# A hybrid trunk layer: another unit of seven products in each of three weight products, and half of their low-half subtractions on GpSimd

## The chip, the core and the metric

The kernel runs on one core of one Trainium2 chip. The time is that of one execution on the device, in microseconds. The kernel before takes 1451.33 us, the median of three runs (1449.8 to 1453.53). One execution was also recorded by the hardware profiler; every duration below is from that record.

## What is computed

One layer of a decoder for 256 tokens of width 2048, in float32. The change touches the step in which two attention branches are merged: columns of the input projection give gates, and the gates weigh the two branches' output projections.

```python
h = rms_norm(x, norm_mix_pre)
# w_in: columns 3392 to 5439 are the gates of branch A, 5440 to 7487 those of branch B
gates = h @ w_in[:, 3392:7488]
g = sigmoid(gates).reshape(B, S, 2, 2048)
merged = g[:, :, 0] * (o_a @ w_o_mla) + g[:, :, 1] * (o_b @ w_o_swa)
y = merged @ w_out
```

`o_b` is the result of the sliding-window attention, `w_o_swa` its 2048x2048 output matrix (`wo_b` in the kernel).

## The kernel before

**Three products for one.** TensorE multiplies in a reduced float32 format (`F32R`). To keep float32 accuracy each operand is split in a high half, rounded to that format, and a low half, the rest. Each product of operands is then three matmuls, high by high, high by low and low by high (`mm3`, L195 to L198). For the weights, `convert` (L150) makes the halves: ScalarE copies the raw row block into `whi` (L161), VectorE subtracts it from the raw one to give `wlo` (L162). The halves go through a ring of four buffers each (`RING = 4`): a conversion waits until TensorE has used the one four before.

**Pairs of column blocks.** `pair_gemm` computes the product of 256 tokens with 1024 columns of weights. Tokens come in two tiles of 128, columns in two blocks of 512, and the 2048 rows of the weights in 16 blocks of 128 rows, taken two by two: eight units. An order string says for each unit of which kind it is:

- `p`, a plain unit: two row blocks, each converted at 128x1024 and multiplied with both token tiles: 2 x 2 x 2 products, 24 matmuls of 128x512.
- `s`, a unit of seven products (Winograd's form of Strassen's scheme): 21 matmuls. It needs sums and differences of the four token blocks, made ahead by `token_sums` (L378 to L388), and of the four weight blocks. GpSimd's queue loads the two row blocks (`gr`, L329 and L330), VectorE makes four 512-wide differences (`weight_sums`, L225 to L232) into `gta` and `gtb`, and four pieces are converted: the odd row block (1024 wide), half of the even one (512), `gta` and `gtb` (1024 each). At the end of the product `end_sums` adds the four sums of seven-product units back (L358 to L364).

**The stage around the change.** First comes `out_b(0)`, a plain product of the first 512 columns of `wo_b`. Then `gate_pair(0, ...)` and `gate_pair(2, ...)`, two pairs for the 2048 gates of branch B, and `out_pair`, a pair for columns 512 to 1535 of `wo_b`. The last 512 columns (`out_b(3)`) follow later, mixed with the next stage. A gate pair ends with four additions from PSUM (L838) and four tanh on ScalarE (L839); `gated` (L796, L797) multiplies the gate with the branch and stores the result from GpSimd's queue. `out_pair` ends with four additions from PSUM (L857) and four `gated`.

**What sets the order.** The instructions of VectorE, ScalarE and SyncE are put in order at build time by a planner; those of TensorE and GpSimd stand in the order of the code. Each engine works through its instructions in that order. `at(t, f)` asks for a piece of work at a tick; a unit of either kind takes two ticks. The token sums of the gates (`x_sums`) and of the output (`o_sums`) are asked for so.

Of the kernel before, what the change touches and what calls it, by code (L numbers as in the profile page):

```python
# [11 lines left out]
F32 = mybir.dt.float32  # L12
F32R = mybir.dt.float32r
# [3 lines left out]
ALU = mybir.AluOpType  # L17
AX = mybir.AxisListType

P = 128  # L20
# [20 lines left out]
def trunk_layer(ctx, tc, x, x_cols_in, conv_cols_in, g_mix_post, g_ffn_post, w_in, w_q, w_kv,  # L41
                sinks, rel, wo_a, wo_b, w_out, w_up, w_down, rope_tab, out):
    nc = tc.nc
    vec, act, pe, pool = nc.vector, nc.scalar, nc.tensor, nc.gpsimd
# [10 lines left out]
    base = ctx.enter_context(tc.tile_pool(name="base", bufs=1))  # L55
    ring = ctx.enter_context(tc.tile_pool(name="ring", bufs=RING))

    def sb(pl, shape, name, dt=F32, tag=None, bufs=None):
        return pl.tile(shape, dt, name=name, tag=tag or name, **({"bufs": bufs} if bufs else {}))
# [12 lines left out]
    def warm_up(n):  # L72
        for i in range(n):
# [7 lines left out]
                       base=0, channel_multiplier=1)  # L81
# [65 lines left out]
        flex[0] = kind  # L147
        turn.update(raw=0, w=0)

    def convert(raw, n, own=None, parts=None, into=None):  # L150
        i = cnt[0]
        cnt[0] += 1
        if into:
            hi, lo = into
        elif own:
            hi, lo = (own.tile([P, 1024], F32R, name=f"w{part}{i}", tag="w" + part) for part in ("hi", "lo"))
        else:
            extra = in_turn("w")
            hi, lo = (ring_tile("w" + part, f"w{part}{i}", F32R, extra) for part in ("hi", "lo"))
        for a, b in parts or ((0, n),):  # L160
            act.copy(hi[:, a:b], raw[:, a:b])  # L161
            vec.tensor_tensor(lo[:, a:b], raw[:, a:b], hi[:, a:b].bitcast(F32), op=ALU.subtract)  # L162
        return hi, lo

    def raw_row(src, n=1024):
        i = cnt[0]
        cnt[0] += 1
        raw = new_raw(f"raw{i}")
        ins = nc.sync.dma_start(raw[:, :n], src)
        if more_raw and more_raw[-1] is raw_x and "rx" not in staged:  # L170
            staged.add("rx")
            tc.keep_in_program_order(ins)
        return raw
# [100 lines left out]
        u, p = (i, 0) if i < NA[0] else (i - NA[0], 1)  # L274
        return park_sums(f"ta{i}_", w_down, 2 * u, 1024 * p, place, t0, **kw)

    def pair_gemm(name, w, k0, c0, order, act_of, s_of, kind, d, place=None, sums=None, parked=None, held=None, into=None, tied=False):

        c11, c12, c21, c22 = c = banks(kind, f"c{name}_")
        q, used = [], set()  # L280
        row = lambda k: w[(k0 + k) * P:(k0 + k + 1) * P, c0:c0 + 1024]
# [6 lines left out]
        chunks, hold = [2 * order.count("p")], len(held) if held else 0  # L288
        left = [order.count("s")]

        def plain(u, last):
            for k in (2 * u, 2 * u + 1):
                chunks[0] -= 1
                w_ = convert(raw_row(row(k)), 1024, into=into(chunks[0]) if hold else None)
                for t in range(NT):
                    if t and chunks[0] < hold:
                        held[hold - 1 - chunks[0]] = (act_of(k, 1), w_)
                        continue
                    for j in range(2):
                        mul(c[2 * t + j], act_of(k, t), half(w_, j),  # L300
                            not (chunks[0] or (t and hold)) and (j == 1 or not left[0]))
                tick()
# [23 lines left out]
        def seven(u, last):  # L326
            s1, s2, s3, s4 = s_of(u)
            even, odd = place()
            pool.dma_start(even, row(2 * u))  # L329
            pool.dma_start(odd, row(2 * u + 1))  # L330
            ta, tb = sums()
            w_ = convert(odd, 1024)
            weight_sums(even, odd, ta, tb, tied)
            if not q:
                q[:] = banks(1 - kind, f"q{name}_")
            q1, q5, q7, q6 = q
            mul(c11, act_of(2 * u + 1, 0), half(w_, 0))
            mul(c12, s4, half(w_, 1))
            w_ = convert(even, 512)
            mul(q1, act_of(2 * u, 0), half(w_, 0), last)  # L340
            w_ = convert(ta, 1024)
            mul(q5, s1, half(w_, 0), last)
            mul(q7, s3, half(w_, 1), last)
            tick()
            w_ = convert(tb, 1024)
            left[0] -= 1
            mul(q6, s2, half(w_, 0), last)
            mul(c21, act_of(2 * u + 1, 1), half(w_, 1))
            tick()
            if last:  # L350
                end_sums()
# [17 lines left out]
        n = order.count("s")  # L369
        plain_of, seven_of = iter(range(n, len(order))), iter(range(n))  # L370
        for i, kd_ in enumerate(order):
            if kd_ == "s":
                u = next(seven_of)
# [336 lines left out]
    for g in range(4):  # L710
        acc = gemm(XH, XL, w_in, 0, KT, C_QS + 512 * g, 512)[0] if g else acc_q0
        swa_q(g, acc)
        b = now[0]
# [47 lines left out]
    acc, _ = gemm(XH, XL, w_in, 0, KT, 0, 512)  # L761
# [4 lines left out]
    acc, _ = gemm(XH, XL, w_in, 0, KT, C_KV, KVR + ROPE)  # L766
# [28 lines left out]
    def gated(j, t, g, o):  # L795
        vec.scalar_tensor_tensor(g, g, 1.0, o, op0=ALU.add, op1=ALU.mult)  # L796
        pool.dma_start(yb_d[j, t], g)  # L797
# [3 lines left out]
    esg, pg = open_pool("pg")  # L801
    xs = {}

    def x_sums(u):
        st = sb(pg, [P, 1024], f"xs{u}", F32R)
        a, m = (sb(pg, [P, 512], f"x{n}{u}", tag="x" + n, bufs=1) for n in "am")
        xs[u] = token_sums(xt[u].bitcast(F32), a, m, st[:, 0:512], st[:, 512:1024])

# [7 lines left out]
    os_ = {}  # L816

    def o_sums(u):
        st = sb(pg, [P, 1024], f"os{u}", F32R)
        a, m = (sb(pg, [P, 512], f"o{n}{u}", tag="x" + n, bufs=1) for n in "am")  # L820
        os_[u] = token_sums(ot[u].bitcast(F32), a, m, st[:, 0:512], st[:, 512:1024])

    def two_pairs(act_of, s_of, w, c0, kind, name, order, tiles):
        d = []

        def result_tiles():
            d[:] = tiles()
            return d

        c = pair_gemm(name, w, 0, c0, order, lambda k, t: tuple(x(k)[:, t * P:(t + 1) * P] for x in act_of),  # L830
                      lambda u: s_of[u], kind, result_tiles, g_place, gate_sums, tied=True)
        return c, d

    def gate_pair(j, kind, tiles, then=lambda t, g: None):
# [26 lines left out]
            finish_out(i)  # L861

    both = sb(base, [P, D], "ob0", tag="sg")
    for t, f in ((0, lambda: x_sums(0)), (3, lambda: x_sums(1)), (6, lambda: o_sums(0)), (10, lambda: x_sums(2)), (28, lambda: o_sums(1))):
        at(now[0] + t, f)
    acc = out_b(0, (pss, "s"))
    for t in range(NT):
        act.copy(both[:, t * 512:(t + 1) * 512], acc[t])
    tb1 = [sb(pg, [P, 512], f"tb1_{t}") for t in range(NT)]
    gate_pair(0, 0, lambda: [x_ for t in range(NT) for x_ in (stg(f"tb0_{t}"), tb1[t])],  # L870
              lambda t, g: gated(0, t, g, both[:, t * 512:(t + 1) * 512]))
    parked_b2 = []
    d = gate_pair(2, 1, lambda: [stg(f"tb{2 + i}_{t}") for t in range(NT) for i in range(2)])
    out_pair((tb1, d[0::2]))
# [152 lines left out]
    b = now[0] + 2  # L1027
# [5 lines left out]
    acc = out_b(3)  # L1033
# [4 lines left out]
    for j in range(4):  # L1038
        acc, _ = gemm(XH, XL, w_in, 0, KT, C_GA + 512 * j, 512)
        if j == 3:  # L1040
            both = sb(base, [P, D], "ta3", tag="sg")
        for t in range(NT):
            g = both[:, t * 512:(t + 1) * 512] if j == 3 else stg(f"ta{j}_{t}")
# [523 lines left out]
    held = [None] * 7  # L1567
# [52 lines left out]
RING = 4  # L1620
A_ORDER = "ppspspsp"
NA_ = A_ORDER.count("s")
GATE_ORDER = "ppspspsp"
OUT_ORDER = "ppsppspp"
B_ORDER = "psspsspssp"
B2_ORDER = "ppsspssppp"
NB2 = B2_ORDER.count("s")
# [74 lines left out]
```

## Time and profile before

| | |
|---|---|
| median of three runs | 1451.33 us |
| the profiled execution, in all | 1448.96 us |
| its span, first to last instruction | 1447.2 us |
| TensorE's mean granted clock | 0.998 |
| two gate pairs, first matmul to first of the output pair | 218.35 to 301.70 us |
| output pair, first to last matmul | 301.9 to 344.5 us |
| low halves on VectorE in the whole span (L162, from `raw`, `gr`, `gta`, `gtb` and others) | 491, 576.0 us |

A line of the profile's timeline gives start, duration, engine, line of the kernel, operation, output<-input without buffer numbers, shape, and in brackets the idle time before it with what ended it. Rows that follow each other without a gap on VectorE overlap a little: the step from one start to the next is shorter than the duration. PE is TensorE's matmul, DVE is VectorE, ACT ScalarE, POOL GpSimd, SP SyncE.

### The profile page before, as it was taken

To read this page: it belongs to the slowest core of one execution; us is meant where nothing else is said; L and a number is where in the kernel's file an instruction comes from. 1 tells how busy PE (TensorE), PEld (TensorE's weight loads), DVE (VectorE), ACT (ScalarE), POOL (GpSimd) and SP (SyncE) were. 2 spreads that over 40 slices of the span, in tenths; PEclk is the share of its full clock that TensorE was granted. 3 is DMA by queue.
4 is the path that set the end of the run, shared out by engine and by line. 5 is a ranking of instruction groups with operands and counts; after the bars stand their busy time and mean duration, and the time that the engine had idled before them with its cause. 6 is when DMAs were issued, how large, how long until landed. Compare 5 with 4: busy or idle time off the path is not lost.

```text
span 1447.2 us, 21393 instructions
## 1 busy us (share of the span) xinstructions
PE 1436.9 (99%) x7497; PEld 1228.8 (85%) x7497; DVE 1175.9 (81%) x2042; ACT 864.7 (60%) x1400; POOL 127.6 (9%) x240
## 2 busy tenths in 40 slices
PE   9999999999999999999999999999999999999997
PEld 7888888888888888888888888888888888888886
DVE  7788898988777775978789888986778787876798
ACT  7588875554555655546566565555656555555673
POOL 2022110000000111100000111100000100010000
PEclk9999999999999999999999999999999999999999
DMA  9655375657876779965666799987988888778965
GB/s 317 203 172 162 105 262 185 215 181 221 260 215 206 239 241 331 345 221 187 219 230 220 267 364 344 325 287 232 319 285 294 284 293 278 256 272 286 355 216 205
DMA packets 162316, 365.45 MB, mean 253 GB/s; under 512 B 21008, under 2 KB 32144, under 8 KB 162208
## 3 DMA queue, kind: packets, MB, share of 16 engines
q1 hardware_dynamic: 138192, 278.82, 57.5%
q0 software_dynamic: 23872, 85.00, 16.8%
q8 instruction: 59, 0.97, 0.3%
q14 instruction: 49, 0.40, 0.1%
q10 hardware_dynamic: 144, 0.26, 0.1%
HBM read 327.29 MB, written 36.75 MB: 252 GB/s over the span
## 4 chain that ended last, share of the span: by engine, by line
PE 55%; DVE 1%; DMA 1%; issue 0%; ACT 0%; DVEq 0%; ACTq 0%
PE ub L1395 10%; PE ua L1395 10%; PE ub L1399 5%; PE ua L1399 5%; PE cd L198 2%; PE cd L196 2%; PE cd L197 2%; PE accg L198 2%; PE accg L196 2%; PE accg L197 2%; PE cdc L198 1%; PE cdc L196 1%; PE cdc L197 1%; PE qd L198 1%; PE qd L196 1%; PE qd L197 1%
## 5 line engine op out<-in xcount | busy, mean ns | idle before, releaser
L161 ACT CAST whi<-raw 128x1024 fp32r<-128x1024 f32 (+2 forms) x491 | 496.7, 1022 | 348.6 <-PE accg L198 70.0
L162 DVE TENSOR_TENSOR wlo<-raw,whi 128x1024 fp32r<-128x1024 f32 (+2 forms) x491 | 576.0, 1186 | 146.2 <-ACT whi L161 139.7
L1395 PE MATMUL ua<-ahl,whi 128*128 128x512 f32 x640 | 154.6, 391 | 0.0
L1395 PE MATMUL ub<-ahl,whi 128*128 128x512 f32 x640 | 154.5, 391 | 0.0
L196 PE MATMUL accg<-whi,ahl 128*128 128x512 f32 (+1 forms) x352 | 137.4, 391 | 0.0
L1395 PEld LDWEIGHTS ua<-ahl,whi 128*128 128x128 f32 x640 | 117.5, 188 | 22.7
L1395 PEld LDWEIGHTS ub<-ahl,whi 128*128 128x128 f32 x640 | 117.5, 188 | 22.7
L198 PE MATMUL accg<-whi,ahl 128*128 128x512 f32 (+1 forms) x352 | 135.6, 385 | 0.0
L197 PE MATMUL accg<-wlo,ahl 128*128 128x512 f32 (+1 forms) x352 | 134.8, 383 | 0.0
L1399 PEld LDWEIGHTS ub<-ahl,wlo 128*128 128x128 f32 x640 | 82.2, 191 | 3.2
L1399 PEld LDWEIGHTS ua<-ahl,wlo 128*128 128x128 f32 x640 | 82.2, 191 | 3.1
L1399 PE MATMUL ua<-ahl,wlo 128*128 128x256 f32 x640 | 83.7, 283 | 0.0
L1399 PE MATMUL ub<-ahl,wlo 128*128 128x256 f32 x640 | 83.2, 283 | 0.0
L198 PEld LDWEIGHTS accg<-whi,ahl 128*128 128x128 f32 x352 | 66.1, 188 | 12.7
L196 PE MATMUL accg<-whi,bhl 128*128 128x512 f32 x192 | 76.0, 396 | 0.0
L197 PEld LDWEIGHTS accg<-wlo,ahl 128*128 128x128 f32 x352 | 66.2, 188 | 10.6
L196 PEld LDWEIGHTS accg<-whi,ahl 128*128 128x128 f32 x352 | 66.1, 188 | 10.6
L198 PE MATMUL accg<-whi,bhl 128*128 128x512 f32 x192 | 75.1, 391 | 0.0
L197 PE MATMUL accg<-wlo,bhl 128*128 128x512 f32 x192 | 75.0, 391 | 0.0
L161 ACT CAST whi<-xraw 128x1024 fp32r<-128x1024 f32 x34 | 35.9, 1055 | 27.5 <-PE ub L1395 11.9
L162 DVE TENSOR_TENSOR wlo<-xraw,whi 128x1024 fp32r<-128x1024 f32 x34 | 41.5, 1220 | 9.8 <-ACT whi L161 9.8
L198 PEld LDWEIGHTS accg<-whi,bhl 128*128 128x128 f32 x192 | 36.0, 188 | 7.6
(692 smaller groups left out, 2920.5 us busy)
## 6 DMA issues: line engine op xcount, KB each, us to landing
raw<-in_ffn_w_up_dram SPq DMA_DIRECT2D x142, 512.0 KB, 4.9
raw<-in_w_in_dram SPq DMA_DIRECT2D x99, 512.0 KB, 4.5
raw<-in_ffn_w_down_dram SPq DMA_DIRECT2D x64, 512.0 KB, 5.7
xraw<-in_ffn_w_up_dram SPq DMA_DIRECT2D x34, 512.0 KB, 5.5
raw<-in_w_o_swa_dram SPq DMA_DIRECT2D x28, 512.0 KB, 5.5
ta_s<-in_ffn_w_down_dram POOLq DMA_DIRECT2D x28, 512.0 KB, 6.8
ta<-ta_s POOLq DMA_DIRECT2D x28, 512.0 KB, 6.5
raw<-ta SPq DMA_DIRECT2D x28, 512.0 KB, 5.0
```

The source lines that it names most:

```text
L161: act.copy(hi[:, a:b], raw[:, a:b])
L162: vec.tensor_tensor(lo[:, a:b], raw[:, a:b], hi[:, a:b].bitcast(F32), op=ALU.subtract)
L196: pe.matmul(o, ah, bh, start=start, stop=False)
L197: pe.matmul(o, ah, bl, start=False, stop=False)
L198: pe.matmul(o, al, bh, start=False, stop=stop)
L1395: pe.matmul(acc[i], hi[:, c], hn[p][:, j * 512:(j + 1) * 512], start=p + j == 0, stop=stop)
L1399: pe.matmul(acc[i][:, 0:256], lo[:, c], hn[p][:, j * 512:j * 512 + 256], start=False, stop=False)
```

## The change

Two order strings change: the gate pairs get four units of seven products in place of three, in the order plain, plain, seven, seven, plain, seven, seven, plain; the output pair gets three in place of two. The additional token sums are made: a fourth for the gates, in a buffer that is free at that time (`rx`), and a third for the output, in the buffer of the first gate sum (`xs0`), once that has been used for the last time. And `convert` takes the engine that subtracts: in these three pairs GpSimd makes the low halves of the odd row blocks, 24 operations of 128x1024, in plain units as in the others. `ob0` is another name for the first half of the same buffer.

```diff
-    def convert(raw, n, own=None, parts=None, into=None):
+    def convert(raw, n, own=None, parts=None, into=None, low=vec):
...
             act.copy(hi[:, a:b], raw[:, a:b])
-            vec.tensor_tensor(lo[:, a:b], raw[:, a:b], hi[:, a:b].bitcast(F32), op=ALU.subtract)
+            low.tensor_tensor(lo[:, a:b], raw[:, a:b], hi[:, a:b].bitcast(F32), op=ALU.subtract)
...
-                w_ = convert(raw_row(row(k)), 1024, into=into(chunks[0]) if hold else None)
+                w_ = convert(raw_row(row(k)), 1024, into=into(chunks[0]) if hold else None, low=low if k % 2 else vec)
...
             ta, tb = sums()
-            w_ = convert(odd, 1024)
+            w_ = convert(odd, 1024, low=low)
...
     def x_sums(u):
-        st = sb(pg, [P, 1024], f"xs{u}", F32R)
+        st = sb(base, [P, 1024], "xs3", F32R, tag="rx") if u == 3 else sb(pg, [P, 1024], f"xs{u}", F32R)
...
     def o_sums(u):
-        st = sb(pg, [P, 1024], f"os{u}", F32R)
+        st = sb(pg, [P, 1024], f"os{u}", F32R, tag="xs0" if u == 2 else f"os{u}")
...
-                      lambda u: s_of[u], kind, result_tiles, g_place, gate_sums, tied=True)
+                      lambda u: s_of[u], kind, result_tiles, g_place, gate_sums, tied=True, low=pool)
...
-    for t, f in (... (10, lambda: x_sums(2)), (28, lambda: o_sums(1))):
+    for t, f in (... (10, lambda: x_sums(2)), (14, lambda: x_sums(3)),
+                 (26, lambda: o_sums(1)), (34, lambda: o_sums(2))):
         at(now[0] + t, f)
...
-GATE_ORDER = "ppspspsp"
-OUT_ORDER = "ppsppspp"
+GATE_ORDER = "ppsspssp"
+OUT_ORDER = "ppspspsp"
```

GpSimd's queue at the beginning of the first gate pair. Before, it holds only the loads of row blocks for seven-product units (`gr`), two for each unit:

```order
L329 DMA gr_2853<-in_w_in_dram 128x1024
L330 DMA gr_2853<-in_w_in_dram 128x1024
L329 DMA gr_2939<-in_w_in_dram 128x1024
L330 DMA gr_2939<-in_w_in_dram 128x1024
L329 DMA gr_3021<-in_w_in_dram 128x1024
L330 DMA gr_3021<-in_w_in_dram 128x1024
```

Now the low halves of odd row blocks stand between them, of plain units (from `raw`) and of the others (from `gr`):

```order
L329 DMA gr_2903<-in_w_in_dram 128x1024
L330 DMA gr_2903<-in_w_in_dram 128x1024
L162 TENSOR_TENSOR wlo_2792<-raw_2789,whi_2791 128x1024
L162 TENSOR_TENSOR wlo_2838<-raw_2835,whi_2837 128x1024
L162 TENSOR_TENSOR wlo_2859<-gr_2853,whi_2858 128x1024
L329 DMA gr_2995<-in_w_in_dram 128x1024
L330 DMA gr_2995<-in_w_in_dram 128x1024
L162 TENSOR_TENSOR wlo_2909<-gr_2903,whi_2908 128x1024
```

Three subtractions stand ahead of the load for the third seven-product unit, and one more ahead of that for the fourth.

VectorE at the first seven-product unit of the first gate pair. Before, between the second token row (`xa`, `xm`, `xs` for the gates, `oa`, `om`, `os` for the output) and the low half of the even row block (from `gr`, 512 wide):

```order
L162 TENSOR_TENSOR wlo_2838<-raw_2835,whi_2837 128x1024
L421 TENSOR_TENSOR os_3238<-om_3240,os_3238 128x512
L162 TENSOR_TENSOR wlo_2859<-gr_2853,whi_2858 128x1024
L230 TENSOR_TENSOR gta_2856<-gr_2853 128x512 x2
L230 TENSOR_TENSOR gtb_2857<-gr_2853,gta_2856 128x512
L162 TENSOR_TENSOR wlo_2877<-gr_2853,whi_2876 128x512
L230 TENSOR_TENSOR gtb_2857<-gr_2853,gtb_2857 128x512
```

Now:

```order
L421 TENSOR_TENSOR xs_2939<-xm_2941,xs_2939 128x512
L384 TENSOR_TENSOR om_3198<-oa_3197 128x128
L385 TENSOR_TENSOR om_3198<-oa_3197 128x128
L386 TENSOR_TENSOR om_3198<-om_3198,oa_3197 128x128
L387 TENSOR_TENSOR om_3198<-oa_3197,om_3198 128x128
L381 TENSOR_TENSOR oa_3397<-bhl_608 128x512
L162 TENSOR_TENSOR wlo_2877<-gr_2853,whi_2876 128x512
L421 TENSOR_TENSOR os_3196<-om_3198,os_3196 128x512
```

The two 1024-wide low halves are gone from here to GpSimd, the four weight sums have moved up, and the fourth gate sum (`xs_2939`) and the beginning of the third output sum (`oa_3397`) stand ahead of the even row's low half; the low half of the second output sum (`os_3196`) has come behind it.

VectorE at the end of the output pair. Before, low halves for the next product (from `raw`) stand between the additions and the gating:

```order
L857 TENSOR_TENSOR udo<-udo,co_3467 128x512
L162 TENSOR_TENSOR wlo_3866<-raw_3863,whi_3865 128x1024
L796 SCALAR_TENSOR_TENSOR tb_0_2765<-tb_0_2765,udo 128x512
L857 TENSOR_TENSOR udo<-udo,co_3468 128x512
L857 TENSOR_TENSOR udo<-udo,co_3469 128x512
L796 SCALAR_TENSOR_TENSOR tb_0_3422<-tb_0_3422,udo 128x512
L796 SCALAR_TENSOR_TENSOR tb_1_2766<-tb_1_2766,udo 128x512
L857 TENSOR_TENSOR udo<-udo,co_3470 128x512
L162 TENSOR_TENSOR wlo_3888<-raw_3884,whi_3887 128x1024
```

Now:

```order
L162 TENSOR_TENSOR wlo_3898<-raw_3895,whi_3897 128x1024
L363 TENSOR_TENSOR udo<-udo,qo_3605 128x512
L364 TENSOR_TENSOR udo<-udo,qo_3605 128x512
L857 TENSOR_TENSOR udo<-udo,co_3507 128x512
L857 TENSOR_TENSOR udo<-udo,co_3508 128x512
L796 SCALAR_TENSOR_TENSOR tb_0_2765<-tb_0_2765,udo 128x512
L796 SCALAR_TENSOR_TENSOR tb_0_3462<-tb_0_3462,udo 128x512
L857 TENSOR_TENSOR udo<-udo,co_3509 128x512
L857 TENSOR_TENSOR udo<-udo,co_3510 128x512
L796 SCALAR_TENSOR_TENSOR tb_1_2766<-tb_1_2766,udo 128x512
L796 SCALAR_TENSOR_TENSOR tb_1_3464<-tb_1_3464,udo 128x512
L162 TENSOR_TENSOR wlo_3916<-raw_3913,whi_3915 128x1024
```

The eight finishing operations stand together, and the third low half of the next product behind all of them.

More of the change, by code (lines that the diff above doesn't have):

```diff
@@ L275, in park_a, with pair_gemm @@
         return park_sums(f"ta{i}_", w_down, 2 * u, 1024 * p, place, t0, **kw)
-    def pair_gemm(name, w, k0, c0, order, act_of, s_of, kind, d, place=None, sums=None, parked=None, held=None, into=None, tied=False):
+    def pair_gemm(name, w, k0, c0, order, act_of, s_of, kind, d, place=None, sums=None, parked=None, held=None, into=None, tied=False, low=vec):
         c11, c12, c21, c22 = c = banks(kind, f"c{name}_")
@@ L863, in trunk_layer @@
     both = sb(base, [P, D], "ob0", tag="sg")
-    for t, f in ((0, lambda: x_sums(0)), (3, lambda: x_sums(1)), (6, lambda: o_sums(0)), (10, lambda: x_sums(2)), (28, lambda: o_sums(1))):
+    ob0 = both[:, 0:1024]
+    for t, f in ((0, lambda: x_sums(0)), (3, lambda: x_sums(1)), (6, lambda: o_sums(0)), (10, lambda: x_sums(2)), (14, lambda: x_sums(3)),
+                 (26, lambda: o_sums(1)), (34, lambda: o_sums(2))):
         at(now[0] + t, f)
@@ L867, in trunk_layer @@
     for t in range(NT):
-        act.copy(both[:, t * 512:(t + 1) * 512], acc[t])
+        act.copy(ob0[:, t * 512:(t + 1) * 512], acc[t])
     tb1 = [sb(pg, [P, 512], f"tb1_{t}") for t in range(NT)]
     gate_pair(0, 0, lambda: [x_ for t in range(NT) for x_ in (stg(f"tb0_{t}"), tb1[t])],
-              lambda t, g: gated(0, t, g, both[:, t * 512:(t + 1) * 512]))
+              lambda t, g: gated(0, t, g, ob0[:, t * 512:(t + 1) * 512]))
     parked_b2 = []
```

## The prediction, made before the changed kernel ran

> **What bounds the kernel now.** I read the page first, then a table by stretches around the three pairs, then the order of single matmuls and of VectorE's instructions inside them.
>
> ```profile
> PE 1436.9 (99%) x7497; PEld 1228.8 (85%) x7497; DVE 1175.9 (81%) x2042; ACT 864.7 (60%) x1400; POOL 127.6 (9%) x240
> 200.00:218.35 18.35, 18.35 (x85) 15.12 (x84) 18.25 (x41) 9.90 (x15) 0.23 (x1) 1.00 0.91 314
> 218.35:301.70 83.35, 83.35 (x366) 68.57 (x365) 73.23 (x90) 47.72 (x54) 7.41 (x14) 1.00 0.62 203
> 301.70:342.50 40.80, 40.80 (x180) 33.61 (x179) 32.08 (x37) 22.47 (x25) 0.00 (x0) 1.00 0.50 149
> ```
>
> The last three lines give, for each stretch, its length, then busy time and count of PE, PEld, DVE, ACT and POOL, the granted clock, the DMA share and GB/s. The two gate pairs run from 218.35 to 301.70 us, the output pair behind them. TensorE is the bound, at full clock; VectorE is busy for 73.23 of 83.35 us there, and GpSimd is nearly idle.
>
> ```profile
> 218.35 0.39 PE L196 MATMUL cg<-whi,ahl 128*128 128x512 f32 x1
> 218.58 0.39 PE L197 MATMUL cg<-wlo,ahl 128*128 128x512 f32 x1
> 229.92 0.40 PE L196 MATMUL cg<-whi,xs 128*128 128x512 f32 x1
> ACT whi L161 <- PE cg L198: 32.2, 26, 2.1
> ```
>
> A matmul lasts 0.39 us but the next one starts after 0.227: the third row is the 52nd matmul of the first gate pair, and (229.92 - 218.35) / 51 = 0.227. The stretch agrees, 83.35 / 366 = 0.228, so TensorE has no gaps to be won here. The last row, from the table of waits, says who waits for whom: the high-half copies on ScalarE wait for TensorE to free a weight buffer. The conversions lead, TensorE follows.
>
> **What is removed.** A plain unit is 24 matmuls (5.45 us), a seven-product unit 21 (4.77 us). Three units change kind, so 9 matmuls go: 9 x 0.227 = **-2.04 us**. This is all that can be gained, since TensorE waits for nothing here.
>
> **What is added to VectorE.** One seven-product unit of before:
>
> ```profile
> 234.24 1.22 DVE L162 TENSOR_TENSOR wlo<-gr,whi 128x1024 fp32r<-128x1024 f32 x1
> 235.37 1.29 DVE L230 TENSOR_TENSOR gta<-gr 128x512 f32<-128x512 f32 x2
> 236.58 0.68 DVE L230 TENSOR_TENSOR gtb<-gr,gta 128x512 f32<-128x512 f32 x1
> 237.18 0.68 DVE L162 TENSOR_TENSOR wlo<-gr,whi 128x512 fp32r<-128x512 f32 x1
> ```
>
> From start to start a 1024-wide low half costs 1.13 us, a 512-wide operation 0.60. A seven-product unit asks of VectorE, without its odd row, 4 x 0.60 + 0.60 + 2 x 1.13 = 5.26 us, a plain unit 1.13. Four of each are 25.6 us against 4 x 4.77 + 4 x 5.45 = 40.9 us of TensorE: if GpSimd worked beside VectorE, all would be hidden.
>
> **What the moved low halves cost.** The trace has 16 GpSimd subtractions of the same kind (L702, 128x256, both inputs in SBUF), and shows what they do to VectorE:
>
> ```profile
> 77.42 1.22 DVE L162 TENSOR_TENSOR wlo<-raw,whi 128x1024 fp32r<-128x1024 f32 x1
> 77.71 1.53 POOL L702 TENSOR_TENSOR bhl<-o,bhl 128x256 fp32r<-128x256 f32 x1 [0.36 <-ACT bhl L701]
> 78.56 0.70 DVE L655 TENSOR_TENSOR mx<-mx,sink 128x4 f32<-128x4 f32 x1
> 79.18 0.74 DVE L424 SCALAR_TENSOR_TENSOR qx<-accg,r1s,qx 128x512 fp32r<-128x512 f32 x1
> 87.30 0.15 DVE L655 TENSOR_TENSOR mx<-mx,sink 128x4 f32<-128x4 f32 x1
> 85.56 0.74 POOL L702 TENSOR_TENSOR bhl<-o,bhl 128x256 fp32r<-128x256 f32 x1 [6.32 <-ACT bhl L701]
> 95.37 1.52 POOL L702 TENSOR_TENSOR bhl<-o,bhl 128x256 fp32r<-128x256 f32 x1 [1.69 <-ACT bhl L701]
> 96.20 1.01 DVE L421 TENSOR_TENSOR ptl<-pt,pth 128x384 fp32r<-128x384 f32 x2
> ```
>
> GpSimd's 0.74 becomes 1.53 when a VectorE operation with two SBUF inputs is already running, and the tiny L655 behind it takes 0.70 instead of 0.15: **the two take turns**. VectorE loses 0.70 - 0.15 = 0.55 us to a 256-wide GpSimd subtraction. The last row (one input in PSUM) runs on beside GpSimd undisturbed. All low halves and weight sums of the pairs have both inputs in SBUF.
>
> For 1024 columns no row stands. Low end: 0.55 plus 768 columns at VectorE's own rate, (1.13 - 0.60) / 512 us each, 1.35 us. High end: four whole isolated instructions, 4 x 0.74 = 2.95. Four times the loss is 2.2; a part of it will be fixed, so I take **2.1 us**.
>
> The Trainium skill (SBUF — State Buffer, section "Who interferes with whom") says that the shared port pair is held for the whole instruction and the loser fully blocks; the trace bears out the blocking but shows VectorE back after 0.55 of 0.74 us, so by the rule to the letter the sum would stand near the high end. The skill's GPSIMD Engine Reference ("Elementwise — side-by-side cycle accounting") gives 4497 ns for a 2048-wide fp32 tensor_tensor; an estimate between that and the 738 ns row is 2.35 us for the instruction at 1024, hold somewhat shorter, and about 1 us more in the sum than mine.
>
> Per unit the two engines then need, in turns: seven-product 5.26 + 2.1 = **7.36 us** against TensorE's 4.77; plain 1.13 + 2.1 = **3.23** against 5.45. A unit behind another seven-product unit cannot be ready in time; plain units win back, but only as far as four weight buffers allow.
>
> *First gate pair.* VectorE is full on entry (18.25 of 18.35 us above) and stays so until here:
>
> ```profile
> 214.78 0.48 DVE L424 SCALAR_TENSOR_TENSOR ckl<-ckT,gmat,ckh 128x256 fp32r<-128x256 f32 x1
> 215.18 0.28 DVE L384 TENSOR_TENSOR xm<-xa 128x128 f32<-128x128 f32 x1
> 215.38 0.28 DVE L385 TENSOR_TENSOR xm<-xa 128x128 f32<-128x128 f32 x1
> 225.83 0.68 DVE L162 TENSOR_TENSOR wlo<-gr,whi 128x512 fp32r<-128x512 f32 x1
> 227.84 1.23 DVE L162 TENSOR_TENSOR wlo<-gta,whi 128x1024 fp32r<-128x1024 f32 x1 [0.72 <-ACT whi L161]
> ```
>
> The even row's low half of the first seven-product unit is ready at 225.83 + 0.68 = 226.5; TensorE wants it after 54 matmuls, 218.35 + 54 x 0.227 = 230.6: 4.1 us of lead. By the new order VectorE has in front of it: three low halves fewer (-3.4), the whole of the fourth token sum (two 512-wide operations and four 128-wide ones of 0.20: +2.0), the first step of the added output sum (+0.6), one weight sum earlier (+0.6), one token low half later (-0.6); GpSimd puts in three of 2.1 (+6.3), beside which the two L424 (0.40 each, an input in PSUM) can run (-0.8). That is 4.7: late by 0.6. From there to the second unit's last row: token work 0.6 + 0.8, two low halves 2.26, a unit 7.36, together 11.0, against 30 matmuls, 6.8: late by 4.2 more. Then plain, seven, seven: 3.23 + 2 x 7.36 = 17.95 against 66 matmuls, 14.98: 3.0. **Sum 7.8 us.**
>
> *Second gate pair.* It starts with two plain units, so the lead comes back, less this: GpSimd's queue now holds two odd rows behind the stores of the gate results, and the finishing work stands between the low halves.
>
> ```profile
> 259.81 1.27 DVE L838 TENSOR_TENSOR tb<-tb,cg 128x512 f32<-128x512 f32 x2
> 262.14 1.28 DVE L796 SCALAR_TENSOR_TENSOR tb<-tb,ob 128x512 f32<-128x512 f32 x2
> ```
>
> From TensorE's start of the pair until the first seven-product unit has three of its rows: two odd rows 4.2, one even 1.13, four sums 2.4, 0.60, 1.13, two L796 1.2, and half of four L838 (PSUM input, 2.4) 1.2: 11.9 against 48 matmuls, 10.9: 1.0. The rest of the unit and the next, 1.13 + 7.36 = 8.5 against 36 matmuls, 8.2: 0.3. Plain, seven, seven as before: 3.0. **Sum 4.3 us.**
>
> *Output pair.* Units alternate: from TensorE's start of the first seven-product unit, 1.13 + 2 x (3.23 + 7.36) = 22.3 against 105 matmuls, 23.8. **Nothing.** At its end the new order sets four L857 and four L796 ahead of the third low half of the next product: 8 x 0.60 + 1.22 = 6.0 against two chunks of 12 matmuls, 5.45: **0.6**.
>
> *Costed at nothing.* Six 512 KB loads go from SyncE's queue to GpSimd's; the engines are 0.62 busy, and the issues wait behind low halves on a queue that needs per pair 8 x 2.3 (the hold and the 0.2 us by which the isolated row is longer) + 8 x 0.53 = 23 of 41 us:
>
> ```profile
> 239.01 0.53 POOL L329 DMA_DIRECT2D gr<-in_w_in_dram  x1 [10.30 <-ACT whi L161]
> DMA to landing us min/median/max: 3.7/4.6/7.2
> ```
>
> The third output sum reuses the first token sum's buffer: its ScalarE copy and VectorE low half wait until TensorE has left that unit. Where TensorE waits for VectorE this is past; if the lead were there, it would shorten it by about one copy and one low half, 0.62 + 0.60. ScalarE gets one and a half copies more per changed unit and has room, 47.72 busy of 83.35 us.
>
> **Sum:** 7.8 + 4.3 + 0.6 - 2.0 = **+10.6 us**. The profiled execution (1447.2 us span, 1448.96 us in all) becomes 1459.6; the median shown, 1451.33, is 2.4 above it, so I forecast **1462 us**. With 1.35 us per moved row the pairs lose 2.6, nothing and 0.6: +1.2 us, 1452.5. With 2.95 they lose 13.8, 9.4, 1.9 and 0.6: +23.7 us, 1475.
>
> **Rivals.** *Beside each other, not slower:* GpSimd's reads leave VectorE alone at this size, or VectorE's lead swallows them; 25.6 of 40.9 us per pair, TensorE never waits, -2.0 us, 1449.3. For it: GpSimd 9% busy, VectorE freed of 24 x 1.13 = 27 us. Against it: 0.70 where 0.15 is usual. It decides from a hold of about 1.2 us downward, where the sum above is nothing. *Short hold:* the fixed part of 0.55 us is large and the hold 1.3 to 1.5: 1452 to 1455. *GpSimd's queue:* in the second pair two odd rows stand behind stores that wait for L796, which waits for ScalarE's tanh (L839).
>
> ```profile
> 261.31 1.33 ACT L839 ACTIVATE tb<-tb,rh 128x512 f32<-128x512 f32 x2
> 263.12 0.55 POOL L797 DMA_DIRECT2D yb_d<-tb  x1 [12.75 <-DVE tb L796]
> ```
>
> If each row starts one gate result later than I count, L838 0.60, tanh 0.66, L796 0.60 and the issue 0.55, that is 2.4 us, twice 4.8: 1467. Before, the store went out a microsecond after its L796 had begun, so I give it little. *The change doesn't do what it says:* excluded by the order for the matmuls, which are 9 fewer.
>
> **How the numbers follow.** Forecast 0.58; short hold 0.16; beside each other 0.16; GpSimd's queue 0.10. The range, 1452 to 1475, takes in the bounds of the hold and the queue, and leaves out mainly the side-by-side case. What a measurement of this kernel can tell from no change is about 0.3%, 4.4 us: slower is above 1455.7. Slower: 0.58 + 0.10 + half of the short hold, 0.76. Same: 0.22. Faster by 4.4 us is beyond the 2.04 us that can go: 0.02.
>
> **What the profile of the changed kernel would show.** If right: GpSimd low halves of over 2 us, longer where they wait; 512-wide weight sums on VectorE stretched well above 0.68; TensorE idle in front of matmuls with `wlo`, most in the second unit of a "ss" and in the first gate pair, little in the output pair; some 95 us instead of 83 for the gate pairs. If wrong: VectorE's rows at 0.68 and 1.22 while GpSimd runs, and no gap on TensorE, which would make the prediction 12 us too long; or gaps that follow DMA waits on `gr`, which would be the queue.

## The result and the profile after

The changed kernel takes **1470.18 us**, the median of four runs (1467.46 to 1471.17), beside 1451.8 (1449.8 to 1453.53) for the kernel before on the same chip. The ratio is 1.0125, with a 95% interval of 1.0109 to 1.0142: slower, by 18.4 us between the medians. That is inside the predicted range and on the predicted side, but 1.7 times the 10.6 us of the sum. The profiled execution took 1471.17 us, with a span of 1469.4.

First the line of engines on the page of the changed kernel:

```profile
PE 1443.0 (98%) x7488; PEld 1227.0 (84%) x7488; DVE 1205.4 (82%) x2048; ACT 868.8 (59%) x1408; POOL 199.5 (14%) x270
```

Then its windows (length, busy time and count of PE, PEld, DVE, ACT and POOL, granted clock, DMA share, GB/s): the two gate pairs, and the whole stage, from the first matmul of the gate pairs to the first weight load for `qn`, one of the products that follow the output pair (the beginning of the last 512 columns of `wo_b` and a smaller product stand between). The fence behind it has that stage in the kernel before.

```profile
218.70:317.99 99.29, 88.17 (x362) 67.15 (x361) 94.53 (x101) 52.54 (x62) 57.33 (x34) 0.98 0.53 168
...
218.74:375.68 156.94, 144.05 (x604) 112.37 (x603) 148.15 (x155) 80.40 (x92) 79.84 (x49) 0.99 0.55 175
```

```profile
218.35:357.85 139.50, 139.50 (x613) 114.72 (x612) 118.34 (x146) 75.74 (x85) 10.65 (x20) 1.00 0.62 197
```

Nine matmuls are gone, as they should be (7497 to 7488). The stage went from 139.50 to 156.94 us, **+17.4**, nearly all of the result. The rest can't be assigned: outside the stage the profiled executions of the kernels below took between 1307.7 us (the kernel before) and 1315.9 (e9). The gate pairs alone, to the first matmul of the output pair, went from 83.6 to 99.25. TensorE filled the stage before, and now stands still for 13 us of it. VectorE went from 118.34 busy to 148.15, although 24 low halves left it (of the 70 in the changed pairs, so about a third; the count of 491 given ahead is of those from `raw` alone): in the gate pairs it is busy for 94.53 of 99.29 us, and so it is the bound there.

The groups of VectorE and GpSimd around the stage (205 to 365 us for VectorE, 196 to 375 for GpSimd; busy time and mean of one, idle before) say why.

```profile
L230 DVE TENSOR_TENSOR gta<-gr 128x512 f32<-128x512 f32 x22 | 35.3, 1640 | 0.0
L162 DVE TENSOR_TENSOR wlo<-raw,whi 128x1024 fp32r<-128x1024 f32 x19 | 27.6, 1455 | 0.5 <-ACT whi L161 0.5
...
L230 DVE TENSOR_TENSOR gtb<-gr,gta 128x512 f32<-128x512 f32 x11 | 11.9, 1082 | 0.0
...
L162 POOL TENSOR_TENSOR wlo<-raw,whi 128x1024 fp32r<-128x1024 f32 x13 | 38.1, 2933 | 42.6 <-ACT whi L161 27.3 <-DVE xm L384 15.2
L162 POOL TENSOR_TENSOR wlo<-gr,whi 128x1024 fp32r<-128x1024 f32 x11 | 30.1, 2735 | 3.9 <-ACT whi L161 3.9
```

A 512-wide weight sum takes 1.640 us in the first group, where 0.68 was usual; these 22 alone lost 22 x (1.640 - 0.68) = 21 us. All groups of VectorE there together are some 40 us above their usual durations, 1.7 us for each of the 24 GpSimd rows, of which VectorE was spared 1.13 each. (A row's usual duration is that of the same operation and shape in the kernel before.) Single rows of the timeline (start, duration) show the turn being taken:

```profile
215.88 2.40 POOL L162 TENSOR_TENSOR wlo<-raw,whi 128x1024 fp32r<-128x1024 f32 x1 [15.23 <-DVE xm L384]
215.93 2.50 DVE L386 TENSOR_TENSOR xm<-xm,xa 128x128 f32<-128x128 f32 x1
...
245.33 2.67 POOL L162 TENSOR_TENSOR wlo<-raw,whi 128x1024 fp32r<-128x1024 f32 x1 [1.41 <-ACT whi L161]
245.65 5.70 DVE L230 TENSOR_TENSOR gta<-gr 128x512 f32<-128x512 f32 x2
247.96 2.84 POOL L162 TENSOR_TENSOR wlo<-gr,whi 128x1024 fp32r<-128x1024 f32 x1
```

A 128-wide L386 that takes 0.28 us elsewhere takes 2.50 beside a GpSimd row of 2.40: VectorE lost 2.22. Where two GpSimd rows followed each other, each of two weight sums waited for one of them: 5.70 for two operations that take 1.28.

The table of waits shows what came of it for TensorE (196 to 375 us: microseconds, times, the longest). Before, this table had no row in the stage.

```profile
PE qg L197 <- DVE wlo L162: 7.5, 9, 1.8
PE cg L197 <- POOL wlo L162: 3.5, 5, 2.0
PE accg L196 <- DVE udo L857: 1.4, 1, 1.4
PE qo L197 <- DVE wlo L162: 0.4, 1, 0.4
```

These are 12.8 us. From start to start TensorE loses more, because each wait costs about 0.26 us beyond the idle time shown: the matmul at 233.11 waits 1.71, starts 2.09 after the one before it, and the next follows after 0.34, where two usual steps are 0.45 together.

### The profile page after: what moved, and what is told of

It is laid out like the page before. It is cut to its first block, busy times and chain, and to the rows that moved or that the text cites. A ratio compares the mean times of both kernels' runs of the same rounds, so it can differ in the third digit from the quotient of the medians.

```text
span 1469.4 us, 21417 instructions
## 1 busy us (share of the span) xinstructions
PE 1443.0 (98%) x7488; PEld 1227.0 (84%) x7488; DVE 1205.4 (82%) x2048; ACT 868.8 (59%) x1408; POOL 199.5 (14%) x270
## 3 DMA queue, kind: packets, MB, share of 16 engines
q0 software_dynamic: 24736, 88.15, 17.4%
## 4 chain that ended last, share of the span: by engine, by line
PE 47%; DVE 5%; DMA 2%; issue 1%; ACT 1%; DVEq 0%; ACTq 0%
PE ub L1397 10%; PE ua L1397 9%; PE ub L1401 5%; PE ua L1401 5%; DVE wlo L162 2%; PE cd L197 2%; PE cd L196 2%; PE cd L198 2%; PE accg L198 1%; PE accg L197 1%; PE accg L196 1%; DMA mr1hi<-in_w_out_dram 1%; DMA raw<-in_ffn_w_down_dram 1%; PE qd L197 1%; PE qd L196 1%
## 5 line engine op out<-in xcount | busy, mean ns | idle before, releaser
L161 ACT CAST whi<-raw 128x1024 fp32r<-128x1024 f32 (+2 forms) x485 | 490.3, 1022 | 339.8 <-PE accg L198 69.4
L162 DVE TENSOR_TENSOR wlo<-raw,whi 128x1024 fp32r<-128x1024 f32 (+2 forms) x472 | 558.1, 1195 | 143.5 <-ACT whi L161 135.9
L197 PEld LDWEIGHTS accg<-wlo,ahl 128*128 128x128 f32 x352 | 66.2, 188 | 10.6
L196 PEld LDWEIGHTS accg<-whi,ahl 128*128 128x128 f32 x352 | 66.2, 188 | 10.6
L162 DVE TENSOR_TENSOR wlo<-xraw,whi 128x1024 fp32r<-128x1024 f32 x34 | 41.5, 1221 | 10.1 <-ACT whi L161 10.0
L162 POOL TENSOR_TENSOR wlo<-raw,whi 128x1024 fp32r<-128x1024 f32 x13 | 38.1, 2933 | 42.6 <-ACT whi L161 27.3
```

What stands on the lines that cost most here:

```text
L162: low.tensor_tensor(lo[:, a:b], raw[:, a:b], hi[:, a:b].bitcast(F32), op=ALU.subtract)
L196: pe.matmul(o, ah, bh, start=start, stop=False)
L197: pe.matmul(o, ah, bl, start=False, stop=False)
```

## The experiments

Each kernel is the changed one with the edit shown (for e9 and e10 it is e3 with the edit shown). The table gives the median, the ratio to the kernel before, run beside it each time (medians of 1450.93 to 1452.29), with its interval, and from the profile of each the length of the stage, with VectorE's busy time in it. The stage is from a single execution each, so differences of a microsecond in it say little. An edit shifts the line numbers behind it: VectorE's low halves are L165 in e3 and e10, L166 in e9, and L163 in e4, where GpSimd's are L165. The stage would take 139.5 - 1.9 = 137.6 us if only the matmuls went.

| kernel | us | ratio | stage | VectorE busy |
|---|---|---|---|---|
| before | 1451.33 | 1 | 139.50 | 118.34 |
| changed | 1470.18 | 1.0125 (1.0109 to 1.0142) | 156.94 | 148.15 |
| e1, VectorE makes all low halves | 1455.89 | 1.0028 (1.0014 to 1.0041) | 143.11 | 134.29 |
| e2, orders of before, GpSimd as changed | 1455.31 | 1.0025 (1.0015 to 1.0035) | 142.42 | 132.38 |
| e3, memset for the GpSimd rows | 1450.79 | 1.0001 (0.9984 to 1.0018) | 137.64 | 108.50 |
| e9, three memsets for each | 1451.83 | 0.9999 (0.9983 to 1.0014) | 137.63 | 108.51 |
| e10, GpSimd copies one input | 1460.42 | 1.0050 (1.0032 to 1.0068) | 147.70 | 123.97 |
| e5, GpSimd in plain units only | 1460.14 | 1.0057 (1.0035 to 1.0079) | 147.41 | 137.06 |
| e11, GpSimd in seven-product units only | 1462.68 | 1.0068 (1.0048 to 1.0088) | 150.39 | 145.69 |
| e4, half of each row on GpSimd | 1466.82 | 1.0099 (1.0073 to 1.0124) | 154.58 | 143.10 |
| e7, token sums at their ticks | 1471.47 | 1.0130 (1.0108 to 1.0152) | 157.91 | 152.18 |
| e8, mixed orders, VectorE makes all | 1456.61 | 1.0030 (1.0018 to 1.0043) | 143.21 | 130.04 |

### Each half of the change alone (e1, e2)

```diff
-                      lambda u: s_of[u], kind, result_tiles, g_place, gate_sums, tied=True, low=pool)
+                      lambda u: s_of[u], kind, result_tiles, g_place, gate_sums, tied=True)
```

> All four parts of the changed kernel stay (orders, additional units, token sums), but VectorE makes the odd rows' low halves again. Theory (the two engines take turns at SBUF, a GpSimd low half takes 2.2 us from VectorE where its own costs 1.13): a seven-product unit then needs 6.39 us of VectorE against 4.77 of TensorE, a plain one 2.26 against 5.45; the first gate pair loses about 1.8 us, the second nothing, the tail 0.6, and 2.0 are won: 1450 to 1454. Rival (the additional units and sums are themselves too much for VectorE, whoever subtracts): still slower by 10 us or more, above 1461.

```diff
-GATE_ORDER = "ppsspssp"
-OUT_ORDER = "ppspspsp"
+GATE_ORDER = "ppspspsp"
+OUT_ORDER = "ppsppspp"
```

> The orders and sums of before (three, three and two units of seven products), but GpSimd makes the 24 low halves of odd rows as in the changed kernel. Theory (turns at SBUF, decided unit by unit): seven and plain units alternate, 10.6 us of turns per pair of units against 10.2 of TensorE, so most is hidden: 1452 to 1457. Rival (GpSimd's queue or its 24 operations as such, wherever they stand): most of the 18 us remains, 1462 or more.

In e2 the token sums are asked for as in the kernel before, too. Alone, each half costs little, 0.28% and 0.25%; together 1.25%. e1 came out 2 us above the range expected of it, and 5 below its rival's; e2 is within its range. The table of waits of e1 in the stage, then that of e2:

```profile
PE qg L196 <- ACT whi L161: 1.7, 3, 0.6
PE qg L197 <- DVE wlo L162: 1.2, 2, 0.7
PE accg L196 <- DVE udo L857: 0.3, 1, 0.3
```

```profile
PE qg L197 <- DVE wlo L162: 1.4, 4, 0.4
```

In e1 TensorE waits three times for a high half, made by ScalarE from a weight sum of VectorE: without GpSimd, too, the second of two seven-product units comes too late.

**VectorE's load adds up, which fits that the times don't.** The orders put 134.29 - 118.34 = 16.0 us on VectorE, GpSimd's rows 132.38 - 118.34 = 14.0 in e2. 118.34 + 16.0 + 14.0 = 148.3, and the changed kernel has 148.15. The stage before had 139.50 - 118.34 = 21 us in which VectorE was idle. Each half by itself uses about half of these and leaves 9 (e1) to 10 (e2). The changed kernel still has 156.94 - 148.15 = 8.8, as much as e1: none of that time could be used for GpSimd's rows, and their 14 us appear in full, 156.94 - 143.11 = 13.8.

### What about the GpSimd rows costs the time (e3, e9, e10, e4)

A memset writes the buffer and reads nothing. In e3 one stands in place of each subtraction:

```diff
-            low.tensor_tensor(lo[:, a:b], raw[:, a:b], hi[:, a:b].bitcast(F32), op=ALU.subtract)
+            if low is pool:
+                pool.memset(lo[:, a:b].bitcast(F32), 0.0)
+            else:
+                vec.tensor_tensor(lo[:, a:b], raw[:, a:b], hi[:, a:b].bitcast(F32), op=ALU.subtract)
```

> As the changed kernel, but in place of the 24 subtractions GpSimd writes zeros into the low halves of the odd rows (memset, which reads nothing from SBUF), so these low halves are left out of the product. Queue, buffers, loads and TensorE's matmuls are the same. Theory (the loss is VectorE shut out while GpSimd reads SBUF): nearly all of it goes, 1449 to 1453, and VectorE's weight sums keep 0.68 us beside GpSimd's work. Rival (odd rows behind loads and stores in GpSimd's queue): at least half of the loss remains, 1460 or more.

A memset is shorter than a subtraction, so e9 makes each three times:

```diff
-                pool.memset(lo[:, a:b].bitcast(F32), 0.0)
+                for _ in range(3):
+                    pool.memset(lo[:, a:b].bitcast(F32), 0.0)
```

> As the run with zeros in place of the 24 subtractions, but GpSimd writes each low half three times, about 2.9 us of GpSimd for each odd row, longer than the subtraction's 2.4. The odd rows' low halves are left out of the product again. Theory (VectorE is shut out because GpSimd reads SBUF): writes shut nobody out, 1449 to 1454. Rival (GpSimd is simply too slow, so TensorE gets the odd rows late): 1462 or more.

The gate pairs of e9 in a window, and behind it its groups of memsets and of weight sums:

```profile
217.76:300.07 82.31, 82.31 (x361) 67.56 (x360) 68.79 (x98) 51.80 (x60) 54.61 (x67) 1.00 0.60 200
```

```profile
L164 POOL MEMSET wlo<- 128x1024 f32 x72 | 67.7, 957 | 47.2 <-PE cg L201 16.0 <-PE accg L201 15.1 <-PE qo L201 14.1
...
L234 DVE TENSOR_TENSOR gta<-gr 128x512 f32<-128x512 f32 x22 | 14.2, 683 | 0.0
```

GpSimd is as busy there as in the changed kernel (54.61 and 57.33 us), its queue carries the same loads and stores behind as long a work, the orders are the same, and the stage is 1.9 us shorter than before: all that the removed matmuls can give. VectorE's weight sums are at 0.683. So neither GpSimd's pace nor its queue is the cause, nor do the orders cost anything while VectorE is spared the odd rows. One more thing differs in e3 and e9: a memset doesn't wait for ScalarE's high half, as the subtraction does, so its low halves can be ready earlier. The next kernel takes that out. The whole kernel doesn't show those 1.9 us: the ratios are 1.0001 and 0.9999, with 2 us or a little more to either side.

One input from SBUF in place of two (the odd rows' low halves are then the rows themselves, so the products aren't those of the layer):

```diff
-                pool.memset(lo[:, a:b].bitcast(F32), 0.0)
+                pool.tensor_copy(lo[:, a:b], raw[:, a:b])
```

> As the changed kernel, but GpSimd copies the odd rows into their low halves (one input from SBUF in place of two), so the low halves of odd rows are replaced by the rows themselves. Theory (any reading by GpSimd takes the turn from VectorE's two-input operations): the turn is shorter with one input, about 1 to 1.3 us, so 1455 to 1461, and VectorE rows beside it are stretched. Rival (only GpSimd instructions with two inputs take turns with VectorE): as with the writes alone, 1449 to 1454.

Rows of GpSimd, VectorE and TensorE from the timeline of e10:

```profile
237.64 3.61 DVE L165 TENSOR_TENSOR wlo<-gtb,whi 128x1024 fp32r<-128x1024 f32 x1
238.14 1.05 POOL L163 CAST wlo<-raw 128x1024 fp32r<-128x1024 f32 x1
239.12 1.05 POOL L163 CAST wlo<-gr 128x1024 fp32r<-128x1024 f32 x1
241.31 0.50 PE L200 MATMUL qg<-wlo,xs 128*128 128x512 f32 x1 [2.02 <-DVE wlo L165]
```

A copy of one input takes its turn as well: a low half that takes 1.22 us elsewhere takes 3.61 across two copies of 1.05, and TensorE waits 2.02 us for just that. The copy, like the memset, doesn't wait for ScalarE, and it lasts about as long (1.05 and 0.96 us); so e10 against e3 shows little but the reading: 147.70 - 137.64 = 10.1 us of stage, with 15.5 more of VectorE's busy time. Here VectorE's load isn't the whole story: with 123.97 us it is busier than before by only 5.6, and yet the stage is 8.2 longer. A turn that falls into the middle of a seven-product unit delays TensorE even where VectorE has time later.

Half as many columns on GpSimd:

```diff
-            low.tensor_tensor(lo[:, a:b], raw[:, a:b], hi[:, a:b].bitcast(F32), op=ALU.subtract)
+            m = (a + b) // 2 if low is pool else b
+            vec.tensor_tensor(lo[:, a:m], raw[:, a:m], hi[:, a:m].bitcast(F32), op=ALU.subtract)
+            if m < b:
+                pool.tensor_tensor(lo[:, m:b], raw[:, m:b], hi[:, m:b].bitcast(F32), op=ALU.subtract)
```

> As the changed kernel, but each odd row's low half is shared: VectorE makes columns 0 to 511, GpSimd columns 512 to 1023. Theory (what VectorE loses grows with the columns that GpSimd reads): hold about 1.1 us and 0.60 of its own against 2.2, so about half way between all on VectorE (1455.9) and the changed kernel (1470.2): 1458 to 1464. Rival (each GpSimd operation costs a fixed turn): 1467 or more.

I had expected the cost to fall with the columns; e4 keeps 15.1 of the 17.4 us in the stage, and its 1466.82 (1463.79 to 1470.83) lies above the theory's range and close to the rival's 1467. The hold did shrink: VectorE's operations there are 21.5 us above their usual durations, 0.9 for each GpSimd row, in place of 1.7, which speaks against a fixed turn. But VectorE got half of each row back, and its load stays at 143.10. Something else shows in its timeline (GpSimd, then TensorE):

```profile
287.67 7.33 POOL L165 TENSOR_TENSOR wlo<-raw,whi 128x512 fp32r<-128x512 f32 x1 [1.41 <-ACT whi L161]
294.97 1.27 POOL L165 TENSOR_TENSOR wlo<-gr,whi 128x512 fp32r<-128x512 f32 x1
...
295.06 0.80 PE L200 MATMUL cg<-wlo,ahl 128*128 128x512 f32 x1 [3.10 <-POOL wlo L165]
295.65 0.63 PE L201 MATMUL cg<-whi,ahl 128*128 128x512 f32 x1
...
300.77 0.63 PE L201 MATMUL cg<-whi,xs 128*128 128x512 f32 x1
```

An operation of 1.27 us stood for 7.33, while VectorE went from one operation to the next without a pause. TensorE waited 3.10 us for it and then ran at about half its pace until 301.2 (the last section). Together this one place is 6 of the 15.1 us, so the time of e4 doesn't decide between its theory and its rival. The changed kernel has one such place, in the second gate pair (GpSimd, VectorE and TensorE):

```profile
291.82 1.21 DVE L162 TENSOR_TENSOR wlo<-raw,whi 128x1024 fp32r<-128x1024 f32 x1
292.17 6.09 POOL L162 TENSOR_TENSOR wlo<-raw,whi 128x1024 fp32r<-128x1024 f32 x1 [1.40 <-ACT whi L161]
292.96 1.28 DVE L230 TENSOR_TENSOR gta<-gr 128x512 f32<-128x512 f32 x2
...
295.37 0.68 DVE L230 TENSOR_TENSOR gtb<-gr,gtb 128x512 f32<-128x512 f32 x1
297.28 2.06 DVE L162 TENSOR_TENSOR wlo<-gta,whi 128x1024 fp32r<-128x1024 f32 x1 [1.23 <-ACT whi L161]
298.31 0.50 PE L197 MATMUL cg<-wlo,ahl 128*128 128x512 f32 x1 [1.97 <-POOL wlo L162]
302.27 1.23 DVE L162 TENSOR_TENSOR wlo<-gtb,whi 128x1024 fp32r<-128x1024 f32 x1 [2.93 <-ACT whi L161]
```

### Which rows (e5, e11)

```diff
-            w_ = convert(odd, 1024, low=low)
+            w_ = convert(odd, 1024)
```

> As the changed kernel, but GpSimd makes the low halves of odd rows in plain units only (13 of 24); in units of seven products VectorE makes them. Theory: seven-product unit 6.39 us, plain unit 3.3; plain, seven, seven need 16.1 against 15.0, the first gate pair loses about 4 us, the second about 0.5, the tail 0.6, less 2.0: 1453 to 1458. Rival (24 GpSimd operations cost 0.8 us each wherever they stand): 13 of 24, about 1462.

```diff
-                w_ = convert(raw_row(row(k)), 1024, into=into(chunks[0]) if hold else None, low=low if k % 2 else vec)
+                w_ = convert(raw_row(row(k)), 1024, into=into(chunks[0]) if hold else None)
```

> The complement of the run with GpSimd in plain units only: GpSimd makes the low halves of odd rows in the 11 units of seven products, VectorE in the plain ones. Theory (what counts is the turns in units that have none to spare): 7.46 us for a seven-product unit, 2.26 for a plain one; dearer per operation than in plain units: 1462 to 1467. Rival (each of the 24 costs the same wherever it stands, (1470.2 - 1455.9) / 24 = 0.6 us): 1462 at most, as with 13 in plain units 1460 to 1463.

Against e1 (143.11), the 13 rows of plain units cost 4.3 us of stage and the 11 of seven-product units 7.3; the sum, 11.6, is near the 13.8 of both. So the cost isn't in one kind of unit: it is 0.33 us per row in the one and 0.66 in the other, which speaks against the rival that each row costs the same. The totals don't decide: e5 (1460.14) lies between its theory's range and its rival's 1462, 2 us from either, and e11 (1462.68) lies in the ranges of both.

### The order of the work (e7, e8)

e7 ties the second and third output sum to their ticks, so that they no longer stand in front of the first gate pair's weight sums; only its call is shown here:

```diff
-        os_[u] = token_sums(ot[u].bitcast(F32), a, m, st[:, 0:512], st[:, 512:1024])
+        os_[u] = token_sums(ot[u].bitcast(F32), a, m, st[:, 0:512], st[:, 512:1024], u > 0)
```

> As the changed kernel, but the second and third output token sums stay at the ticks at which they are asked for (bound to the order of the program) in place of being drawn ahead of the first seven-product unit's low halves. Theory (the first gate pair is late on entry by what stands ahead of it): about 3 us of VectorE less ahead of the first unit, some of it paid later: 1466 to 1469. Rival (the entry does not matter, only the doubled units): 1470 to 1471.

The theory that this is worth 1 to 4 us in the whole fell; the rival came out, within half a microsecond. From start to start TensorE loses 7.2 us in the first gate pair (10.4 in the changed kernel), but 11.1 in the second (7.0), where those sums now stand; the waits in the stage, in its table, are 8.4 us for VectorE's low halves in twelve places, in place of 7.5 in nine:

```profile
PE qg L197 <- DVE wlo L162: 8.4, 12, 1.1
PE cg L197 <- POOL wlo L162: 3.1, 4, 1.8
```

There is no row of 6 us on GpSimd in this run, and it is as slow. Here, in a stage whose bound is VectorE, moving its work changed where TensorE waits, and not how long.

e8 tries for a version that gains: VectorE makes all low halves, one unit of seven products is added in the second gate pair and one in the output pair, nowhere two in a row, and the sums come late as in e7.

```diff
-                      lambda u: s_of[u], kind, result_tiles, g_place, gate_sums, tied=True, low=pool)
+                      lambda u: s_of[u], kind, result_tiles, g_place, gate_sums, tied=True)
...
-        c, d = two_pairs((XH, XL), xs, w_in, C_GB + 512 * j, kind, f"g{j}", GATE_ORDER, tiles)
+        c, d = two_pairs((XH, XL), xs, w_in, C_GB + 512 * j, kind, f"g{j}", GATE_ORDER if j else "ppspspsp", tiles)
...
-GATE_ORDER = "ppsspssp"
+GATE_ORDER = "spspspsp"
```

> A version without GpSimd arithmetic that avoids two units of seven products in a row: first gate pair as before (three), second gate pair seven, plain, seven, plain, seven, plain, seven, plain (four), output pair with three, VectorE makes all low halves, later output sums as in the run before. Theory: 6 matmuls less, 1.4 us, and VectorE needs 8.7 us per seven and plain unit against 10.2 of TensorE: 1449 to 1452, at best 0.1% faster than before. Rival (every additional seven-product unit costs as in the run with all on VectorE, 5 us for three): 1454 or more.

It doesn't gain, 1.0030: 1456.61 us lies above the 1449 to 1452 expected and in the rival's range. The second pair now begins with a seven-product unit, whose chain of weight sum, copy and low half starts too late:

```profile
PE cg L196 <- ACT whi L161: 1.3, 1, 1.3
PE qg L196 <- ACT whi L161: 1.1, 2, 0.6
```

No version that beats the kernel before was found. e3 and e9 bound what is to be had: with the low halves of the odd rows for nothing, the stage gains 1.9 us, too little for these runs to tell from none in the whole.

## Why the prediction was right, and where it was too small

From start to start at the usual 0.227 us, TensorE's loss can be put beside each term (the counted matmuls of the changed kernel's timeline; the terms are rounded):

| term | predicted | measured |
|---|---|---|
| nine matmuls | -2.0 | -2.0 |
| first gate pair: even row of the first seven-product unit | 0.6 | 2.0 |
| ... to the end of the second unit | 4.2 | 4.8 |
| ... plain, seven, seven | 3.0 | 3.6 |
| second gate pair: first two seven-product units | 1.3 | 2.7 |
| ... plain, seven, seven | 3.0 | 4.3 |
| output pair | 0 | 0.7 |
| the end of it | 0.6 | 1.5 |
| sum | 10.6 | 17.6 |

- **The mechanism held.** GpSimd's operations that read SBUF and VectorE's that read two inputs from it take turns, and VectorE becomes the bound. e3 and e9 show it, with the same orders and, in e9, the same GpSimd time without reads: TensorE has no gap. e10 beside e3 shows that it is the reading. The rival *side by side* is refuted for subtractions and for copies; *GpSimd's queue* is refuted by e9, and in the changed kernel no wait of VectorE or ScalarE in the stage ends with a load of `gr`; the change does what it says.
- **The hold** was put at 2.1 us. A single row shows 2.22, the mean over the stage is 1.7. This term was not too small. The range reached up to 1475 for a hold of 2.95 us, which no row shows: that 1470.18 lies inside it is in part luck, since it needed room that was left for another cause.
- **The step that failed** is the count of a unit's need as VectorE's own work and the turns alone, and with it the sentence that at a hold of about 1.2 us "the sum above is nothing". A low half on VectorE costs 1.13, so e1 is the case to compare, and its stage is 143.11 - 137.6 = 5.5 us above what the removed matmuls would give. The traces show two things that the sums leave out. In e1 TensorE waits 1.7 us for ScalarE: the second of two seven-product units is a chain of weight sum on VectorE, copy on ScalarE and low half on VectorE. In the changed kernel no wait of TensorE is for ScalarE. There VectorE, which the sums never let idle, is idle for 8.8 us of the stage, 4.2 of it before the two low halves at 297.28 and 302.27 shown above, because ScalarE's copies ahead of them waited for TensorE to free a weight buffer; in the second of these waits TensorE itself stood until 298.31 for GpSimd's row. The four weight buffers were named in the prediction but had no price in its sum. How the 7.0 us between 10.6 and 17.6 divide between such waits and the terms below wasn't measured. The two copies:

```profile
296.20 1.04 ACT L161 CAST whi<-gta 128x1024 fp32r<-128x1024 f32 x1 [2.17 <-PE cg L198]
301.19 1.05 ACT L161 CAST whi<-gtb 128x1024 fp32r<-128x1024 f32 x1 [3.94 <-PE cg L198]
```

- **First unit, 0.6 against 2.0.** The two L424 were to run beside GpSimd, for 0.8 us less; but GpSimd's first row started at 215.88, when VectorE was already at L386, and cost its full 2.22. No GpSimd row ran beside either L424, which is 0.8 of the 1.4 us; the three rows took 2.2 each in place of 2.1, 0.3 more.
- **To the second unit, 4.2 against 4.8:** here a part of the loss is TensorE's own clock, told below.
- **Second pair:** the largest single loss, 2.1 us, is the matmul at 298.31, behind the GpSimd row that was kept out from 292.17 on. That GpSimd could be kept out for 6 us wasn't in the sum.
- **The end of the output pair** was late for another reason than stated: not the next product's third low half, but its first matmul, which waits for the first of the additions from PSUM (L857):

```profile
362.07 0.47 PE L196 MATMUL accg<-whi,bhl 128*128 128x512 f32 x1 [1.38 <-DVE udo L857]
```

**Open:** what decides who has the next turn. VectorE kept it from 291.82 over six operations without a pause, and two GpSimd copies in a row went ahead of one low half at 237.64 of e10, although the profile has that low half start 0.5 us before the first copy. At 245.33 the two took turns one by one. No run tested this by itself. Why e10, with so little load on VectorE, loses as much as e5 is shown for one place of 2.02 us only.

## What to carry to other kernels

Moving an elementwise operation to an idle engine is no relief where the two engines take turns at SBUF, as here: compare the time that the busy engine is spared (1.13 us) with the time that it is held (1.7 to 2.2), and try it with a memset of the same length, which shows what the move would give if the reads were free (and with a copy, which adds a read). Two edits that each look nearly free may feed on the same idle time; add up the busy time of the engine that will be the next bound, and see how much of the stage is left. And a unit's need isn't only the sum of its parts on one engine: where a chain crosses to another engine and back, or the buffers between two engines run out, the waits are to be added.

## What the runs showed of the hardware

**GpSimd can be kept waiting by VectorE for several operations**, 6.09 us for a row of 2.4 and 7.33 for one of 1.27, and a low half of VectorE by two GpSimd copies in a row (3.61 us in place of 1.22, e10). Memsets on GpSimd (0.957 us for 128x1024) left VectorE's weight sums at 0.683 us. The Trainium skill (SBUF — State Buffer, "SBUF: two separate sides") says that whichever starts first has the port pair for the whole instruction, and, under "Who interferes with whom", of VectorE's operations with two inputs from SBUF that they contend with GpSimd operations that read SBUF and not with those that only write. e9 agrees with the second, and the loss of 2.22 us to a row of 2.40 with the first; that one engine may go on for several instructions is more than it says.

**A wait of 2 us can halve TensorE's clock for longer than it lasts.** In the first gate pair of the changed kernel TensorE waited 1.71 and 1.82 us within 3 us, and then stepped at 0.43 us where 0.227 is usual:

```profile
233.11 0.50 PE L197 MATMUL qg<-wlo,ahl 128*128 128x512 f32 x1 [1.71 <-DVE wlo L162]
...
235.91 0.79 PE L197 MATMUL qg<-wlo,xs 128*128 128x512 f32 x1 [1.82 <-DVE wlo L162]
236.50 0.63 PE L198 MATMUL qg<-whi,xs 128*128 128x512 f32 x1
236.93 0.63 PE L196 MATMUL qg<-whi,xs 128*128 128x512 f32 x1
```

The window from 235 to 240 us has a granted clock of 0.66:

```profile
235.00:240.00 5.00, 3.70 (x9) 2.49 (x10) 5.00 (x4) 0.74 (x2) 2.78 (x1) 0.66 0.57 203
```

Those steps add about 1 us that no wait in the table shows. In e10 the wait of 2.02 us is followed, a microsecond later, by some 3 us at that step:

```profile
242.66 0.63 PE L199 MATMUL cg<-whi,ahl 128*128 128x512 f32 x1
243.09 0.63 PE L200 MATMUL cg<-wlo,ahl 128*128 128x512 f32 x1
...
245.22 0.63 PE L199 MATMUL cg<-whi,ahl 128*128 128x512 f32 x1
245.65 0.49 PE L200 MATMUL cg<-wlo,ahl 128*128 128x512 f32 x1
```

In e4 the wait of 3.10 us was followed at once by 6 us at that step, with a granted clock of 0.54 from 294 to 299 us; in e7 two waits of 1.14 and 1.76 us, which end at 303.04 and 306.46, were followed by some 3 us. The wait of 1.97 us at 298.31 in the changed kernel had no such sequel, nor had one of 1.70 in e5. The Trainium skill (TensorE: Matmul & The Clock Gate, "Part 1: The HAM clock gate (the "warmup" mystery)") says that the clock goes by the activity in a free-running window of some 3.4 us. That one wait has a sequel and another of the same length none, and that a sequel lasts 3 us (6 in e4), agrees with it; that it takes a whole idle window, as its table has it, does not: 2.02 us were enough.
